# A hybrid RWKV / convolution backbone on one core: priority for three kinds of evictions, and modulation loads behind the last store

## The chip, the cores and the metric

The kernel runs on one core of a Trainium2 chip. The metric is the device time of one execution in microseconds. The engines named below are TensorE (PE in the profile), VectorE (DVE), ScalarE (ACT), GpSimd (POOL) and SyncE (SP, which only issues DMA transfers here).

## The reference

Two layers over 512 latent tokens with a prefix of 256 context tokens, model width 1024. Layer 0 is a time mixing of RWKV-7 kind (16 heads of 64, a scan in both directions) beside a gated short convolution; layer 1 is a Conformer module. Both layers are modulated by a vector that comes from the conditioning. Cut to what matters:

```python
shift, scale, gate = jnp.split(s_lat @ mod_w[i] + mod_b[i], 3, axis=-1)
h = rms_norm(x, g_pre[i]) * (1.0 + scale[:, None]) + shift[:, None]
# layer 0
r, k, v, za, bg, cg, xb, zb = jnp.split(h @ w_in, EVEN_SPLITS, axis=-1)   # context: hc @ w_in
# rwkv_prep: k = k + (centred_shift(k) - k) * mu, and so r, v
def step(S, inp):
    r_t, w_t, k_t, v_t, kk_t, a_t = inp
    sa = jnp.einsum("bhvk,bhk->bhv", S, -kk_t)
    S = (S * w_t[:, :, None, :] + sa[..., None] * (kk_t * a_t)[:, :, None, :]
         + v_t[..., None] * k_t[:, :, None, :])
    return S, jnp.einsum("bhvk,bhk->bhv", S, r_t)
_, S_f, S_b = rwkv_seq(rwkv_prep(hc, rc, kc, vc, *rw), zero, zero, ...)   # context gives the states
ya, _, _ = rwkv_seq(rwkv_prep(h, r, k, v, *rw), S_f, S_b, ...)            # latents start from them
yb = bg * dwconv(cg * xb, sc_w, seg_len)
y = jnp.concatenate([ya * silu(za), yb * silu(zb)], axis=-1) @ w_out
x = x + gate[:, None] * rms_norm(y, g_post[i])
# layer 1: a = u * sigmoid(gl); dwconv of 31 taps; layer_norm; silu(a) * silu(z) @ w_out
```

## The kernel before

The scan is done in chunks of 64 tokens. For each pair of heads (one 128-row block p of the channels) and each direction z, products between keys and receptances within a chunk are made by TensorE into the PSUM tiles `pa` (L677 to L680; `pal` in the profile for latents), and VectorE multiplies them with a mask into `E` (L682). The keys are transposed by TensorE into `pb` and copied by ScalarE into `BKt` (L695). The triangular system within a chunk is solved on VectorE in `solve`: 31 pairs of a product into `xtmp` and a sum into `Y` (L739, L741), each after the last. `merge` (L747 to L766) then puts the inverse together: transposes on VectorE into `kdm` and `am`, two groups of small matmuls into `uh`, and copies into `E`. After that comes the chain (`chain_ctx`, `chain_lat`): a sequence of small dependent steps over the chunks, with matmuls into `zo` and `uh`.

There are 12 stages: s = 0 to 3 run the chains of the context (four blocks, two head pairs each), s = 4 to 11 those of the latents (one head pair each). While the chain of stage s runs, the stage also prepares s + 1 and s + 2: the letters of `STAGE` (L35) name the pieces, S for solve, M for merge, L for the vector work of the preparation (`light`), H for the `pa` and `pb` work (`heavy`), F for fills (projections of receptance and of gate za that lie between the chain's steps; in the latents' stages also the output normalisation `finish`), C for the convolution branch with its gate zb. A scheduler sets the order on each engine: it takes instructions by priority, in the order in which they are written where nothing else is said; `tc.high_priority()` puts an instruction ahead of all others that are ready, and `tc.issue_after(x)` forbids an instruction a place before x. Engines then run their lists strictly in order, and wait at their head.

The projections of the context and latents go through `project` (L443): load two halves of a weight block by SP (`wr` and the block's letters: `wrv`, `wrk`), split each into a high part on ScalarE (`wh`, L129) and a remainder on VectorE (`wl`, L130), then 24 matmuls for the context (`pc...`) and 24 for the latents (`pl...`), which are evicted with the token shift by `shifted`: one ScalarE operation (L437) and two of VectorE (L438, L440). The result of the latents, `lk`, `lv` or `lr`, is stored to the scratch tensor `psp` by a DMA that GpSimd issues (L458).

The modulation of layer 1 and the gate of layer 0 are worked out in the start-up and the first context stages by `rest` (L950 to L976): 17 steps, of which each multiplies four 128x512 pieces of `mod_w` (two matmul columns each, into `uh`, later `mpb`) and then issues the four loads of the step after next, from GpSimd (those of the first steps from SP). The pieces lie in turn in `mwb...` (borrowed from four later tiles; from the ninth step on in `ectx`) and `mwr`. `prep_ctx` calls `rest` after each projection of a block's half, and `lora` (L378), which makes the low-rank decay and rate projections `pwl`, `pal` and `pwc`, after each second of its eight steps.

## Time and profile before

| | |
|---|---|
| median of 3 runs | 1388.19 us (1388.19 to 1389.88) |
| the profiled execution | 1392.7 us, span 1390.9 us |
| mean granted TensorE clock | 0.992 |
| start-up: loads, modulation, first projections, low-rank projections | 0 to about 110 us |
| first context chain to last | up to 482 us |
| latents' chains | from 482 us, some 58 us a stage |
| output projection and layer 1 | to the end |

The profile's page lists busy time by engine, the chain of work that ended last, and the costliest groups of instructions; the trace behind it answers for any stretch. A row of the timeline reads: start, duration, engine, line, operation, tile written <- tiles read, and in brackets the time the engine stood idle before, and what ended it. A row of waits reads: engine, what waited, on what; us in total, times, longest. A row of windows has the busy time and count of PE, weight loads, DVE, ACT and POOL in a stretch, then the granted clock as a share of full speed, the busy share of the DMA engines and GB/s.

### The profile page before, as it was taken

What the parts mean: (1) busy time and instruction counts of PE and PEld (TensorE: products, weight loads), DVE (VectorE), ACT (ScalarE), POOL (GpSimd) and SP (SyncE); (2) the same over time, 40 slices, a digit from 0 to 9 for tenths busy, and PEclk for the clock granted to TensorE, in tenths of its full rate; (3) what the DMA queues carried; (4) which work ended last, traced back from release to release, by engine and by line L of the source; (5) the groups of instructions that cost most, each with busy time, mean ns of one, the idle gap of its engine ahead of it and who ended that gap; (6) DMA issues with size and microseconds to landing.
All of it is one profiled execution on the core that took longest, in us unless ns stands there. A gap on an engine that the chain in (4) does not pass through costs nothing.

```text
span 1390.9 us, 29758 instructions
## 1 busy us (share of the span) xinstructions
PE 1337.1 (96%) x11925; PEld 995.2 (72%) x11925; DVE 985.3 (71%) x2304; ACT 745.3 (54%) x1509; POOL 127.4 (9%) x263
## 2 busy tenths in 40 slices
PE   6989999999899999999999999999999999999998
PEld 2646777777677766676666676677777787788886
DVE  5846879868999599989999998557654653644323
ACT  6536366546756566665666755547742432554222
POOL 4123200001111010101101000010000000000000
PEclk9999999999999999999999999999999999999999
DMA  9855521222323312223222221578621322133232
GB/s 333 254 190 190 189 77 57 87 79 86 88 90 101 99 63 79 70 65 88 82 73 70 76 70 57 183 238 290 222 62 61 121 64 58 61 112 101 91 103 79
DMA packets 139756, 158.55 MB, mean 114 GB/s; under 512 B 15504, under 2 KB 104224, under 8 KB 139498
## 3 DMA queue, kind: packets, MB, share of 16 engines
q1 hardware_dynamic: 123152, 106.47, 24.7%
q0 software_dynamic: 15856, 49.12, 10.8%
q8 instruction: 94, 1.54, 0.5%
q10 hardware_dynamic: 608, 1.06, 0.2%
q14 instruction: 46, 0.37, 0.1%
HBM read 138.33 MB, written 18.28 MB: 113 GB/s over the span
## 4 chain that ended last, share of the span: by engine, by line
PE 66%; DVE 16%; ACT 6%; issue 6%; DMA 5%; SPq 0%; POOL 0%; DVEq 0%; ACTq 0%; POOLq 0%
PE pu L57 10%; PE pz L57 6%; PE f L57 6%; PE uh L57 4%; PE zol L57 4%; PE pcg L57 4%; PE o L57 4%; PE plk L57 3%; PE pxb L57 3%; PE plr L57 2%; PE plv L57 2%; PE pzb L57 2%; DVE E L682 2%; PE pck L57 1%; PE zoc L57 1%
## 5 line engine op out<-in xcount | busy, mean ns | idle before, releaser
L57 PE MATMUL o<-wh,y 128*128 128x512 f32 x248 | 79.7, 397 | 0.0
L739 DVE TENSOR_TENSOR xtmpl<-Xl,Yl 128x126 f32<-128x126 f32 (+22 forms) x248 | 61.9, 250 | 2.8
L741 DVE TENSOR_TENSOR Yl<-Yl,xtmpl 128x126 f32<-128x126 f32 (+22 forms) x248 | 61.9, 250 | 2.7
L1257 ACT CAST ah<-a 64x512 fp32r<-64x512 f32 x32 | 19.8, 618 | 72.6 <-DVE a L1252 72.2
L57 PE MATMUL zol<-UV,E 64*64 64x64 f32 (+1 forms) x1024 | 54.0, 221 | 0.0
L57 PEld LDWEIGHTS o<-wh,y 128*128 128x128 f32 x248 | 45.9, 188 | 9.5
L57 PE MATMUL o<-wl,y 128*128 128x512 f32 x124 | 49.6, 400 | 2.0 <-DVE wl L130 2.0
L57 PE MATMUL pal<-ARl,BKl 64*128 64x128 f32 x512 | 45.7, 298 | 5.8 <-DVE E L682 5.2
L57 PE MATMUL zol<-Hl,ARl 64*64 64x64 f32 x896 | 50.2, 230 | 0.7 <-DVE Hl L854 0.4
L847 ACT COPY UV<-uh 64x128 f32<-64x128 f32 x128 | 33.3, 260 | 32.5 <-PE uh L57 25.0
L57 PEld LDWEIGHTS zol<-Hl,ARl 64*64 64x64 f32 x896 | 34.9, 133 | 20.0 <-issue 15.1
L130 DVE TENSOR_TENSOR wl<-wr,wh 128x1024 fp32r<-128x1024 f32 x28 | 34.2, 1223 | 20.6 <-ACT wh L129 20.5
L57 PEld LDWEIGHTS pal<-ARl,BKl 64*128 64x128 f32 x512 | 36.1, 193 | 16.9 <-issue 10.2
L57 PEld LDWEIGHTS uh<-UV,BKt 128*64 128x64 f32 x704 | 26.3, 137 | 30.3 <-ACT UV L847 23.4
L1252 DVE TENSOR_TENSOR a<-pu,a 128x512 f32<-128x512 f32 x16 | 11.0, 690 | 47.7 <-PE pu L57 45.4
L57 PEld LDWEIGHTS zol<-UV,E 64*64 64x64 f32 (+1 forms) x1024 | 42.2, 136 | 2.8 <-ACT UV L847 2.1
L682 DVE TENSOR_TENSOR E<-pal,maskE 128x512 f32<-128x512 f32 x64 | 43.0, 682 | 0.5 <-PE pal L57 0.3
L1209 DVE SCALAR_TENSOR_TENSOR pr<-px,dbe,What 119x512 f32<-119x512 f32 x32 | 22.6, 747 | 26.6 <-PE px L57 26.6
L129 ACT CAST wh<-wr 128x1024 fp32r<-128x1024 f32 x28 | 29.6, 1057 | 21.3 <-PE o L57 10.7
L854 DVE SCALAR_TENSOR_TENSOR Hl<-uh,PCl,HPl 128x64 f32<-128x64 f32 x112 | 26.4, 277 | 19.4 <-PE uh L57 9.2
L57 PE MATMUL uh<-UV,BKt 128*64 128x64 f32 x704 | 36.3, 232 | 3.3 <-ACT UV L847 2.0
L57 PEld LDWEIGHTS uh<-Ol,E 64*64 64x64 f32 x512 | 19.9, 133 | 24.5 <-ACT Ol L841 17.3
(996 smaller groups left out, 4206.1 us busy)
## 6 DMA issues: line engine op xcount, KB each, us to landing
wr<-in_ev_w_out_dram SPq DMA_DIRECT2D x28, 512.0 KB, 5.2
mwr<-in_mod_w_dram POOLq DMA_DIRECT2D x28, 256.0 KB, 4.3
wrv<-in_ev_w_in_dram SPq DMA_DIRECT2D x16, 256.0 KB, 3.1
ectx<-in_mod_w_dram POOLq DMA_DIRECT2D x16, 256.0 KB, 4.2
wrr<-in_ev_w_in_dram SPq DMA_DIRECT2D x16, 256.0 KB, 2.9
wrza<-in_ev_w_in_dram SPq DMA_DIRECT2D x16, 256.0 KB, 2.8
wrcg<-in_ev_w_in_dram SPq DMA_DIRECT2D x16, 256.0 KB, 2.8
wrxb<-in_ev_w_in_dram SPq DMA_DIRECT2D x16, 256.0 KB, 3.0
```

The lines of the kernel that those rows point to most:

```text
L57: env["pe"] = T.matmul(o, lhsT, rhs, start=start, stop=stop)
L129: S.copy(hi, raw)
L130: env["lo"].tensor_tensor(out=lo, in0=raw, in1=hi, op=ALU.subtract)
L682: st["ev"].append(V.tensor_tensor(out=E[:, h, z * NLAT + c0 : z * NLAT + c0 + m, :], in0=pas[h], in1=maskE[:, z * (1 + h) : z * (1 + h) + ...
L739: V.tensor_tensor(out=tv, in0=X[:, :i, i : i + 1].to_broadcast([P, i, m]), in1=Y[:, i : i + 1, c0:].to_broadcast([P, i, m]), op=ALU.mult)
L741: V.tensor_tensor(out=Y[:, :i, c0:], in0=Y[:, :i, c0:], in1=tv, op=ALU.add)
L847: u_ = S.copy(UV[ZR[1 - h], i : 2 * nch - i : 2 * nch - 1 - 2 * i, ZR[h]], uh[ZR[1 - h], 0:2, :])
L854: h_ = V.scalar_tensor_tensor(out=Hn[:, z, :], in0=uh[:, 2 + z, :], scalar=PC[z][:, i : i + 1], in1=HP[:, z, :], op0=ALU.mult, op1=ALU.add)
L1209: V.scalar_tensor_tensor(out=pr[s][:NPROD], in0=px[s][:NPROD], scalar=dbe[:, 0:1], in1=What[:, n * 512 : n * 512 + 512], op0=ALU.add, op1= ...
L1252: V.tensor_tensor(out=a, in0=pp[1], in1=a, op=ALU.mult)
L1257: S.copy(ahl[s][hr], a[hr])
```

## The change

No instruction is added or taken away on any engine; only their order changes. Four parts:

- Modulation. `lora` leaves out its first call of `rest`, and `prep_ctx` for block 0 makes one more, between the context's and the latents' matmuls of v1. GpSimd's loads for the steps may not be issued before the store of the projection written last (`env["store"]`).
- The evictions of receptance projections (`which` is 0) get high priority.
- The masked evictions into `E` get high priority in the latents' stages.
- The copies into `BKt` get high priority in the latents' stages.

`fills` takes a slice, and a stage letter f would hold later `pa` groups behind a part of the fills. No entry of `STAGE` has an f, so this does nothing.

```diff
@@ lora
-            if kt % 2:
+            if kt % 2 and kt > 1:
                 between()
@@ project
-        shifted(pl, rl, p, which)
-        nc.gpsimd.dma_start(psp[p, which], rl)
+        with nullcontext() if which else tc.high_priority():
+            shifted(pl, rl, p, which)
+        env["store"] = nc.gpsimd.dma_start(psp[p, which], rl)
@@ prep_ctx
-                project(p, which, st[nm][:, cs], inner)
+                project(p, which, st[nm][:, cs], inner if b or (p, which) == (1, 2) else None)
@@ heavy, pa
-                with anchored(an, ha[gi if lat else 2 * gi]):
+                with anchored(an, ha[gi if lat else 2 * gi]), after(st.get("hold") if gi else None):
...
-                        st["ev"].append(V.tensor_tensor(
+                        with tc.high_priority() if lat else nullcontext():
+                            st["ev"].append(V.tensor_tensor(
@@ heavy, pb
-                    st["ev"].append(S.copy(st["BKt"][z][:, :, ZR[h]], pbs[h]))
+                    with tc.high_priority() if lat else nullcontext():
+                        st["ev"].append(S.copy(st["BKt"][z][:, :, ZR[h]], pbs[h]))
@@ rest
-                    nc.gpsimd.dma_start(home(g, q), src)
+                    with tc.issue_after(env["store"].ins):
+                        nc.gpsimd.dma_start(home(g, q), src)
@@
-    sts = [prep_ctx(0, rest)]
+    sts = [prep_ctx(0, rest, inner=rest)]
```

The order on GpSimd in the start-up, before; `lk_559`, `lk_625` and `lv_705` are the latents' projections k0, k1 and v0, whose stores these are:

```order
L976 DMA mwbtanhl_113<-in_mod_w_dram 128x512
L976 DMA mwbtanhl_114<-in_mod_w_dram 128x512
L458 DMA psp<-lk_559 128x512
L976 DMA mwbxal_115<-in_mod_w_dram 128x512
L976 DMA mwbxal_116<-in_mod_w_dram 128x512
L458 DMA psp<-lk_625 128x512
L976 DMA mwr_504<-in_mod_w_dram 128x512
L976 DMA mwr_503<-in_mod_w_dram 128x512
L976 DMA mwr_502<-in_mod_w_dram 128x512
L976 DMA mwr_501<-in_mod_w_dram 128x512
L458 DMA psp<-lv_705 128x512
```

And now:

```order
L459 DMA psp<-lk_559 128x512
L459 DMA psp<-lk_625 128x512
L980 DMA mwbtanhl_113<-in_mod_w_dram 128x512
L980 DMA mwbtanhl_114<-in_mod_w_dram 128x512
L980 DMA mwbxal_115<-in_mod_w_dram 128x512
L980 DMA mwbxal_116<-in_mod_w_dram 128x512
L459 DMA psp<-lv_705 128x512
L980 DMA mwr_504<-in_mod_w_dram 128x512
L980 DMA mwr_503<-in_mod_w_dram 128x512
L980 DMA mwr_502<-in_mod_w_dram 128x512
L980 DMA mwr_501<-in_mod_w_dram 128x512
```

Four loads that stood ahead of and between the two stores of lk now stand behind both, and four more behind the store of lv.

TensorE in the same place, now: the end of the context's matmuls of v1 (`pcv`) and the beginning of the latents' (`plv`); before, the four matmuls on mwb stood behind the 24 of `plv`, right ahead of the four on mwr:

```order
L57 MATMUL pcv_730<-hctx,wlv_726 128x256
L57 MATMUL uh_125<-mwbtanhl_113,s_71 2x512
L57 MATMUL uh_125<-mwbtanhl_114,s_71 2x512
L57 MATMUL uh_125<-mwbxal_115,s_71 2x512
L57 MATMUL uh_125<-mwbxal_116,s_71 2x512
L57 MATMUL plv_766<-hlh_117,whv_719 128x512
L57 MATMUL plv_766<-hll_118,whv_719 128x512
```

One step of the modulation has moved from behind `plv` to ahead of it.

VectorE in a latents' stage (the second), around the last two masked evictions of a head pair, before; `xtmpl` and `Yl` are the solve, `orq` is the output normalisation, and the shape of a solve step shrinks from step to step (here from 5x14 to 4x14):

```order
L741 TENSOR_TENSOR Yl_5628<-Yl_5628,xtmpl_5629 128x5x14
L499 TENSOR_TENSOR orq_5984<-orq_5984 128x8
L682 TENSOR_TENSOR E_4157<-pal_5907,maskE 128x512
L739 TENSOR_TENSOR xtmpl_5629<-Xl_5627,Yl_5628 128x56
L682 TENSOR_TENSOR E_4157<-pal_5906,maskE 128x512
L741 TENSOR_TENSOR Yl_5628<-Yl_5628,xtmpl_5629 128x4x14
```

And now:

```order
L742 TENSOR_TENSOR xtmpl_5629<-Xl_5627,Yl_5628 128x91
L499 TENSOR_TENSOR orq_5984<-orq_5984 128x8
L130 TENSOR_TENSOR wlzb_6148<-wrzb_6146,whzb_6147 128x512
L744 TENSOR_TENSOR Yl_5628<-Yl_5628,xtmpl_5629 128x7x13
L500 TENSOR_TENSOR orq_5984<-orq_5984 128x8
L525 TENSOR_TENSOR lwll_6537<-lwrl_6531,lwhl_6536 128x512
L684 TENSOR_TENSOR E_4157<-pal_5907,maskE 128x512
L684 TENSOR_TENSOR E_4157<-pal_5906,maskE 128x512
```

The two evictions stand next to each other, and the solve has come to its 7x13 step there, where it had come to its 5x14 step before.

## The prediction

> **What bounds the kernel now.** I read the page's busy shares and its chain first, then TensorE's waits stretch by stretch, then the timeline where a wait was long.

> ```profile
> span 1390.9 us, 29758 instructions
> PE 1337.1 (96%) x11925; PEld 995.2 (72%) x11925; DVE 985.3 (71%) x2304; ACT 745.3 (54%) x1509; POOL 127.4 (9%) x263
> PE 66%; DVE 16%; ACT 6%; issue 6%; DMA 5%; SPq 0%; POOL 0%; DVEq 0%; ACTq 0%; POOLq 0%
> ```

> TensorE is busy 96% of the span, and the change leaves its work as it is. So only its idle time (1390.9 - 1337.1 = 53.8 us) and time at a lower clock can be won. Two stretches hold the waits that the edits aim at: the start-up with the context stages, 60 to 482 us, and the latents' stages, 482 to 880 us. After 880 us the order of the work stays. TensorE's waits in the first stretch (total, times, longest):

> ```profile
> PE plv L57 <- DVE lv L440: 4.7, 3, 3.6
> PE pal L57 <- DVE E L682: 3.9, 1, 3.9
> ```

> And in the second:

> ```profile
> PE pbl L657 <- ACT BKt L695: 2.8, 5, 1.0
> PE uh L57 <- DVE aml L748: 2.7, 4, 1.0
> PE pal L57 <- DVE E L682: 1.3, 2, 1.0
> PE pbl L657 <- DVE E L682: 0.6, 2, 0.4
> PE pvl L57 <- ACT BKt L695: 0.4, 1, 0.4
> ```

> **Part 1, the modulation steps at the start.** GpSimd's queue first, then SP's, then how long the value weights' transfers took:

> ```profile
> 62.04 1.09 POOL L976 DMA_DIRECT2D mwbtanhl<-in_mod_w_dram  x2 [12.44 <-PE uh L57]
> 63.13 0.55 POOL L458 DMA_DIRECT2D psp<-lk  x1
> 63.67 1.07 POOL L976 DMA_DIRECT2D mwbxal<-in_mod_w_dram  x2
> 65.11 0.55 POOL L458 DMA_DIRECT2D psp<-lk  x1 [0.38 <-ACT ectx L387]
> ```

> ```profile
> 63.93 1.63 SPq L126 DMA_DIRECT2D wrv<-in_ev_w_in_dram  x2
> ```

> ```profile
> DMA to landing us min/median/max: 3.3/8.0/8.5
> ```

> Four modulation loads and two stores are in flight when the weights of v1 (wrv) are issued. These take 8.0 to 8.5 us, against 3.3 for a wrv later. What follows, in order of time:

> ```profile
> 72.42 0.62 ACT L129 CAST whv<-wrv 128x512 fp32r<-128x512 f32 x1 [5.06 <-DMA wrv<-in_ev_w_in_dram]
> 73.56 2.13 POOL L976 DMA_DIRECT2D mwr<-in_mod_w_dram  x4 [7.90 <-PE uh L57]
> 73.79 13.11 SPq L126 DMA_DIRECT2D wrk<-in_ev_w_in_dram  x4
> 74.30 0.48 PE L57 MATMUL pcv<-hctx,whv 128*128 128x256 f32 x2 [1.02 <-DVE vc L440]
> 78.01 0.62 ACT L129 CAST whk<-wrk 128x512 fp32r<-128x512 f32 x1 [4.11 <-DMA wrk<-in_ev_w_in_dram]
> 78.53 0.68 ACT L437 ACTIVATE lv<-plv,omu 128x512 f32<-128x512 f32 x1
> 80.05 0.75 DVE L440 SCALAR_TENSOR_TENSOR lv<-plv,hmu,lv 128x511 f32<-128x511 f32 x1
> 80.94 0.76 PE L57 MATMUL plv<-hlh,whv 128*128 128x512 f32 x1 [3.56 <-DVE lv L440]
> 81.51 0.63 PE L57 MATMUL plv<-hll,whv 128*128 128x512 f32 x1
> 84.03 0.39 PE L57 MATMUL plv<-hll,whv 128*128 128x512 f32 x1
> 88.00 0.60 PE L57 MATMUL uh<-mwbtanhl,s 128*2 128x512 f32 x2
> 89.83 1.13 PE L57 MATMUL pwl<-ectx,w 128*128 128x512 f32 x2
> ```

> The late wrv holds the cast at 72.42; only then does SP get a buffer for wrk (73.79), which travels beside four mwr loads; ScalarE stands at the cast of wrk until 78.01, and lv's eviction is queued behind it in ScalarE's order. lv frees the PSUM tile that plv(v1) needs. So TensorE idles 1.02 us at pcv and 3.56 us at plv. And it pays a second time, as the granted clock shows:

> ```profile
> 66.00:70.00 4.00, 4.00 (x23) 3.42 (x22) 2.35 (x4) 0.92 (x2) 0.00 (x0) 1.00 0.93 247
> 78.00:82.00 4.00, 1.05 (x3) 0.90 (x4) 2.98 (x5) 1.57 (x3) 0.55 (x1) 0.82 0.74 229
> 82.00:86.00 4.00, 4.00 (x15) 3.21 (x14) 0.19 (x1) 0.62 (x1) 0.00 (x0) 0.75 0.18 66
> ```

> (The last three numbers of a row are granted clock, DMA share and GB/s.) From 80.94 to 84.03 seven matmuls take 3.09 us; the other 17 up to 88.00 take 3.97, 0.233 each, so the seven lose 3.09 - 1.63 = 1.46. A later modulation group waits too:

> ```profile
> 95.19 0.60 PE L57 MATMUL uh<-mwbtanhl,s 128*2 128x512 f32 x2
> 96.44 1.02 PE L57 MATMUL uh<-mwbxal,s 128*2 128x512 f32 x2 [0.21 <-DMA mwbxal<-in_mod_w_dram]
> 97.39 1.12 PE L57 MATMUL pwl<-ectx,w 128*128 128x512 f32 x2
> ```

> It takes 2.20 us; in eight-matmul groups without a wait, as 88.00 with mwr behind it to 89.83, two take 1.83, 0.92 each. So 1.28 is wait. Removable in all: 1.02 + 3.56 + 1.46 + 1.28 = 7.3 us.

> What the changed order does: no load is added, all four move behind the second lk store, to about 65.2 to 67.3. wrv then shares the DMA engines with stores alone. I estimate 3.3 to 5 us for it (above the later wrv's time, below half of 8.5 plus overlap): landed by 69, its subtraction done by 70, wrk issued there rather than at 73.79 and landed by 75 (4.1 us as now, 78.01 less 73.79). lv, two casts' and two shifts' time later (78.01 to 80.80 now, 2.8 us), is through at 77.5. pcv starts when TensorE is free, at 73.28 (74.30 - 1.02). The four matmuls on mwb, now ahead of plv(v1), fill 0.9 us of what was idle; their loads, even at the 8.5 us of the slowest row, are in by 75.8, and the group comes at 76.4 (73.28 and the 3.08 us that pcv takes, from 74.30 to 80.94 - 3.56). So plv(v1) starts near 77.6 at full clock, which leaves 0.3 us idle. The mwr loads now stand behind the store of lv (81.34 now, 77.6 then) in GpSimd's queue instead of ahead of it; with 4 us of travel the last lands near 83.7, when plv(v1) has just ended (77.6 + 24 x 0.233 = 83.2): 0.5 to 1.0 us of new wait, I take 0.8. The loads into ectx further on are also put whole behind stores; bounded by 0 and the 1.28 of the row above, I take 0.3. **Net: -7.3 + 0.3 + 0.8 + 0.3 = -5.9 us**, bounds -7.3 and -2.2 (the last under rival B).

> [...]

> **Part 2, receptance evictions.** 8 fills of one ScalarE and two VectorE operations (0.75 us each by the lv row) move ahead of others in the context stages, where TensorE's order hardly changes. Value 0, bounds -1 and +1.5 (one pair in the way of one chain step).

> **Part 3, the context stage with the 3.9 us wait.** VectorE there:

> ```profile
> 377.50:381.00 3.50, 0.05 (x2) 0.00 (x0) 3.50 (x11) 1.06 (x3) 0.08 (x1) 0.99 0.71 187
> ```

> It is busy all 3.50 us while TensorE waits. Taking the evictions first puts the rest of its queue (the last BK products, then the merge) later by their 4 x 0.68; the wait changes its place rather than goes. Value -0.4, bounds -3.9 and +2.

> **Part 4, the latents' evictions and copies.** The two groups on VectorE:

> ```profile
> L739 DVE TENSOR_TENSOR xtmpl<-Xl,Yl 128x126 f32<-128x126 f32 (+22 forms) x248 | 61.9, 250 | 2.8
> L682 DVE TENSOR_TENSOR E<-pal,maskE 128x512 f32<-128x512 f32 x64 | 43.0, 682 | 0.5 <-PE pal L57 0.3
> ```

> Evictions in pairs, with a solve step (0.25) no longer between, and BKt copies first on ScalarE aim at 2.8 + 1.3 + 0.6 + 0.4 = 5.1 us of waits. Half of these are waits for an operation that starts late for lack of its inputs; I take -2.5. In return the solve is two to three steps (up to six operations, 1.5 us) later at the fourth pair, and TensorE's merges stand later in its order, with fewer zb matmuls (0.23 each) between the last one and the next chain. Where aml is already last (four stages, 2.7 us) more is waited: +1.5, bounds 0 and +10.5 (1.5 in each of seven stages). **Net -1.0.** One more term is the clock:

> ```profile
> 537.00:597.00 60.00, 57.29 (x830) 41.29 (x830) 55.71 (x167) 37.40 (x89) 6.73 (x12) 0.96 0.27 79
> 590.00:592.50 2.50, 2.35 (x94) 2.11 (x96) 2.42 (x5) 1.92 (x4) 0.00 (x0) 1.00 0.17 67
> 592.50:599.00 6.50, 6.50 (x126) 5.89 (x121) 5.28 (x16) 3.75 (x8) 0.00 (x0) 0.51 0.28 83
> ```

> Here no wait was over 1.0 us (the longest of pbl on BKt), yet after a run of transposes, two merges and the output's transposes, without a zb matmul (128x512) between, the clock was 0.51 for 6.5 us: up to 6.5 x 0.49 = 3.2 us. In the new order such a run is gone from this stage and comes together in another. Value 0, bounds -3.2 and +3.2 for each further stage.

> [...]

> **The sum:** -5.9 + 0 - 0.4 - 1.0 = -7.3 us. The profiled execution took 1392.7 us (1.8 around its span), 4.5 above the median of 1388.19; I take the same difference off the median: 1380.9.

> **The rivals.** A, more is won: the 5.1 us all go, the merges have cover (in most stages aml is ready before TensorE comes), the low clock of 592 us does not come again: -5.9 - 5.1 - 3.2 = -14.2, 1374. Against it: VectorE is busy 55.71 of 60 us in that row, so it has little room.

> B, the loads collide all the same: the second wrv is issued by 65.6 (63.93 + 1.63), just as the four loads now start, the DMA engines were busy 0.93 of the time with this traffic (row 66.00:70.00), and if that wrv still lands near 73 and wrk with it, lv stays where it is. Then only the group's 0.92 in the idle time and the 1.28 are won: -2.2, and with part 4 unsure, 1386: no change that can be told. [...] For the forecast speaks that pcv begins with the first half of the weights, issued before the loads.

> C, slower: the solve becomes what TensorE waits for. Place: the merge (aml, then E) ahead of the next chain in seven stages; price 1.5 us a stage, 10.5 in all, with Part 1 won: -5.9 + 10.5 = +4.6, 1392.8. It outweighs the start-up from 5.9/7 = 0.84 us a stage. For it: VectorE's 93% in the stage above. Against: the waits for aml are 0.7 on average now and the merges are scheduled later with it.

> D, the clock halves in two further latents' stages: -7.3 + 6.4 = -0.9, 1387.3.

> **How the numbers follow.** Chances: forecast 0.50, A 0.14, B 0.16, D 0.06, C 0.14. A measurement tells 0.2%, 2.8 us. The forecast (1377 to 1385) and A are faster: 0.64; B and D same: 0.22; C slower: 0.14. The range leaves out the outer part of A and most of C: 1373.5 to 1391.

> **What would show it.** Right: wrv under 6 us, plv(v1) within 1 us of the modulation group at clock 1.0, the chain of the first context stage 5 to 6 us earlier; waits of pbl and pal on BKt and E halved, those on aml up. Wrong: wrv still at 8 us (B), waits on aml over 8 us in all or chain starts waiting for E (C), clock rows near 0.5 in other latents' stages (D).

## The result, and the profile after

| | before | changed |
|---|---|---|
| median of 5 runs | 1388.19 us (1383.39 to 1390.31) | 1399.02 us (1395.87 to 1401.13) |
| profiled execution, span | 1392.7, 1390.9 us | 1400.05, 1398.3 us |
| mean granted clock | 0.992 | 0.989 |

The ratio is 1.0075, with a 95% interval of 1.0048 to 1.0102: slower by about 10.8 us, where 7.3 us less were forecast. (Ratios, here and below, compare the fast executions of both kernels and are not quotients of the medians shown.) The page of the changed kernel, span, busy time by engine and chain:

```profile
span 1398.3 us, 29732 instructions
PE 1345.5 (96%) x11925; PEld 999.3 (71%) x11925; DVE 986.1 (71%) x2304; ACT 742.8 (53%) x1509; POOL 127.1 (9%) x263
PE 71%; DVE 12%; ACT 7%; issue 5%; DMA 4%; POOL 0%; SPq 0%; DVEq 0%; ACTq 0%; POOLq 0%
```

TensorE is busy 8.4 us longer (1337.1 before) with the same matmuls: some of them ran slower. The start-up went largely as foreseen. The changed kernel's timeline, with SP's issue of wrv, ScalarE's cast of wrk and the moved modulation group:

```profile
63.43 1.63 SPq L126 DMA_DIRECT2D wrv<-in_ev_w_in_dram  x2
...
73.66 0.62 ACT L129 CAST whk<-wrk 128x512 fp32r<-128x512 f32 x1 [4.16 <-DMA wrk<-in_ev_w_in_dram]
...
75.73 0.60 PE L57 MATMUL uh<-mwbtanhl,s 128*2 128x512 f32 x2
```

The transfers of wrv, and the window that stood at 0.82 of the clock before:

```profile
DMA to landing us min/median/max: 2.8/3.3/3.8
```

```profile
78.00:82.00 4.00, 4.00 (x19) 3.32 (x18) 0.69 (x1) 0.62 (x1) 3.77 (x8) 1.00 0.85 281
```

wrv lands in 2.8 to 3.8 us instead of 8.0 to 8.5, the cast of wrk comes 4.35 us earlier, and TensorE is busy throughout this window at full clock. The first group on ectx begins at 117.48 instead of 123.68. But that is the last good news. The group on mwr right behind plv, and two later groups on ectx, each of which takes 1.04 us where it waits for nothing, wait for loads:

```profile
82.39 2.59 PE L57 MATMUL uh<-mwr,s 128*2 128x512 f32 x8
...
130.44 2.34 PE L57 MATMUL mpb<-ectx,s 128*2 128x512 f32 x8
...
161.29 2.06 PE L57 MATMUL mpb<-ectx,s 128*2 128x512 f32 x8
```

And TensorE's waits in the latents' stages, 482 to 886 us:

```profile
PE uh L57 <- DVE aml L751: 4.9, 5, 1.5
PE pal L57 <- DVE E L684: 3.1, 7, 1.1
PE pbl L658 <- DVE E L684: 2.1, 5, 0.7
PE pbl L658 <- ACT BKt L698: 1.8, 4, 0.7
PE uh L57 <- ACT UV L850: 1.6, 6, 0.4
PE uh L57 <- DVE Pml L764: 1.3, 2, 0.7
PE po L57 <- DVE Ol L890: 1.0, 4, 0.4
```

The waits on BKt fell from 2.8 to 1.8, but those on E, whose priority was raised, rose from 1.3 + 0.6 to 3.1 + 2.1, and those on the merge's inputs (aml, Pml) from 2.7 to 6.2. The timelines of VectorE and TensorE show both in one stage:

```profile
640.96 0.16 DVE L499 TENSOR_TENSOR orq<-orq 128x8 f32<-128x8 f32 x1
642.19 0.75 DVE L927 SCALAR_TENSOR_TENSOR yb<-cx,hcol,yb 128x512 f32<-128x512 f32 x1 [1.07 <-ACT yb L925]
642.86 1.28 DVE L684 TENSOR_TENSOR E<-pal,maskE 128x512 f32<-128x512 f32 x2
...
644.19 1.16 PE L57 MATMUL pal<-ARl,BKl 64*128 64x128 f32 x16 [1.14 <-DVE E L684]
...
652.40 0.18 DVE L744 TENSOR_TENSOR Yl<-Yl,xtmpl 128x16 f32<-128x16 f32 x1
652.50 2.02 DVE L736 STREAM_TRANSPOSE Xl<-Nt 128x1024 f32<-128x1024 f32 x1
654.40 1.01 DVE L750 STREAM_TRANSPOSE kdml<-Yl 128x512 f32<-128x512 f32 x1
655.45 0.71 DVE L751 STREAM_TRANSPOSE aml<-kdml 128x512 f32<-128x512 f32 x1
...
656.22 1.53 PE L57 MATMUL uh<-aml,E 32*32 32x32 f32 x64 [1.54 <-DVE aml L751]
```

The pair of evictions stands right behind yb, which waits 1.07 us for ScalarE: high priority gave it a place in the order, not a way past a waiting head, and TensorE waits 1.14 us for E. And the solve ends at 652.40, so late that the next solve's 2.0 us transpose Xl stands ahead of the merge; TensorE waits 1.54 us for aml there. The whole of the latents, from the first chain's start to the last one's, before and changed (sums over the seven stages; the first two numbers are length and TensorE's busy time):

```profile
sum 396.00, PE 381.73 PEld 269.83 DVE 358.06 ACT 245.51 POOL 39.01; mean PE 54.53 PEld 38.55 DVE 51.15 ACT 35.07 POOL 5.57
```

```profile
sum 403.70, PE 385.87 PEld 272.11 DVE 358.74 ACT 243.61 POOL 38.93; mean PE 55.12 PEld 38.87 DVE 51.25 ACT 34.80 POOL 5.56
```

Of the 7.7 us more, idle time is 17.83 - 14.27 = 3.6; the other 4.1 are busy time, most of it at a lower clock. Windows of the changed kernel, in pairs:

```profile
537.35:540.75 3.40, 2.13 (x70) 1.65 (x71) 2.84 (x7) 3.12 (x6) 0.77 (x2) 1.00 0.28 83
540.75:544.15 3.40, 3.40 (x36) 1.78 (x38) 2.75 (x6) 1.29 (x3) 0.37 (x1) 0.50 0.29 100
653.40:656.80 3.40, 1.86 (x55) 1.32 (x49) 3.32 (x5) 1.90 (x4) 0.57 (x1) 1.00 0.28 81
656.80:660.20 3.40, 3.40 (x46) 2.85 (x40) 3.08 (x7) 2.83 (x5) 0.56 (x1) 0.50 0.28 95
```

In both pairs 3.40 us at full clock, in which TensorE was busy 63 and 55% of the time, are followed by 3.40 us at 0.50 of it. After 482 us the changed kernel has four of these (540.75, 656.80, 769.45, 834.30, each 3.4 us), the kernel before one of 6.85 us (592.55). Counting half of such time as lost, that is 6.8 against 3.4: +3.4 us. So 3.6 + 3.4 of the 7.7 are accounted for. A ledger of the two profiled executions, by marks on TensorE, in us:

| stretch | before | changed | |
|---|---|---|---|
| up to the first group on ectx | 123.7 | 117.5 | -6.2 |
| to the third context chain (s = 2) | 158.9 | 163.5 | +4.6: among it a new half-clock stretch of 6.85 us at 247.2 (3.4) and the groups on ectx (1.3 + 1.0) |
| to the fourth (s = 3) | 129.1 | 128.3 | -0.8 |
| to the first latents' chain | 70.7 | 73.4 | +2.7: idle 1.7 to 4.0 |
| the latents' chains | 396.0 | 403.7 | +7.7 |
| the rest, to the end of the span | 512.5 | 511.9 | -0.6 |

### The profile page after: what moved, and what is told of

It is laid out like the page before. It is cut to its first block, busy times and chain, and to the rows that moved or that the text cites. A ratio compares the mean times of both kernels' runs of the same rounds, so it can differ in the third digit from the quotient of the medians.

```text
span 1398.3 us, 29732 instructions
## 1 busy us (share of the span) xinstructions
PE 1345.5 (96%) x11925; PEld 999.3 (71%) x11925; DVE 986.1 (71%) x2304; ACT 742.8 (53%) x1509; POOL 127.1 (9%) x263
## 3 DMA queue, kind: packets, MB, share of 16 engines
q10 hardware_dynamic: 608, 1.06, 0.2%
## 4 chain that ended last, share of the span: by engine, by line
PE 71%; DVE 12%; ACT 7%; issue 5%; DMA 4%; POOL 0%; SPq 0%; DVEq 0%; ACTq 0%; POOLq 0%
PE pu L57 13%; PE pz L57 6%; PE f L57 6%; PE uh L57 5%; PE zol L57 4%; PE pxb L57 4%; PE pcg L57 3%; PE plk L57 3%; PE plv L57 3%; PE pzb L57 2%; PE o L57 2%; PE pza L57 2%; DMA wr<-in_ev_w_out_dram 2%; PE plr L57 1%; PE pck L57 1%
## 5 line engine op out<-in xcount | busy, mean ns | idle before, releaser
L57 PE MATMUL o<-wh,y 128*128 128x512 f32 x248 | 79.6, 397 | 0.0
L57 PE MATMUL zol<-UV,E 64*64 64x64 f32 (+1 forms) x1024 | 54.2, 222 | 0.1
L57 PEld LDWEIGHTS o<-wh,y 128*128 128x128 f32 x248 | 46.0, 188 | 9.5
L57 PE MATMUL pal<-ARl,BKl 64*128 64x128 f32 x512 | 44.6, 296 | 7.8 <-DVE E L684 3.8
L57 PE MATMUL zol<-Hl,ARl 64*64 64x64 f32 x896 | 50.2, 230 | 0.7 <-DVE Hl L857 0.6
L57 PE MATMUL o<-wl,y 128*128 128x512 f32 x124 | 49.5, 399 | 1.3 <-DVE wl L130 1.3
L57 PEld LDWEIGHTS zol<-Hl,ARl 64*64 64x64 f32 x896 | 35.0, 133 | 20.4 <-issue 16.5
L57 PEld LDWEIGHTS pal<-ARl,BKl 64*128 64x128 f32 x512 | 35.0, 191 | 18.9 <-DVE E L684 9.7
L57 PEld LDWEIGHTS uh<-UV,BKt 128*64 128x64 f32 x704 | 26.4, 137 | 28.5 <-ACT UV L850 23.1
L57 PEld LDWEIGHTS zol<-UV,E 64*64 64x64 f32 (+1 forms) x1024 | 42.6, 137 | 2.4 <-ACT UV L850 2.0
L129 ACT CAST wh<-wr 128x1024 fp32r<-128x1024 f32 x28 | 29.6, 1057 | 20.7 <-DMA wr<-in_ev_w_out_dram 10.4
L57 PE MATMUL uh<-UV,BKt 128*64 128x64 f32 x704 | 36.3, 232 | 2.1 <-ACT UV L850 1.6
L57 PEld LDWEIGHTS uh<-Ol,E 64*64 64x64 f32 x512 | 20.0, 133 | 25.0 <-ACT Ol L844 18.9
```

Of the source, the lines that this page charges most:

```text
L57: env["pe"] = T.matmul(o, lhsT, rhs, start=start, stop=stop)
L129: S.copy(hi, raw)
```

## The experiments

Every time is a median against the kernel before on the same chip, which stood at 1386.6 to 1387.7 us. Theory 1 was at first: the masked evictions are the loss, since they push the solve back. Rival theories: the receptance evictions (2), and half-clock stretches that any shift moves about (3).

### One part of the change at a time

```diff
e1, the modulation's hunks:
+            if kt % 2 and kt > 1:
+        env["store"] = nc.gpsimd.dma_start(psp[p, which], rl)
+                project(p, which, st[nm][:, cs], inner if b or (p, which) == (1, 2) else None)
+                    with tc.issue_after(env["store"].ins):
+    sts = [prep_ctx(0, rest, inner=rest)]
e2, project:  +        with nullcontext() if which else tc.high_priority():
                  shifted(pl, rl, p, which)
e3, heavy:    +        with tc.high_priority() if lat else nullcontext():
                  st["ev"].append(V.tensor_tensor(out=E[...], ...))
e4, heavy:    +        with tc.high_priority() if lat else nullcontext():
                  st["ev"].append(S.copy(st["BKt"][z][:, :, ZR[h]], pbs[h]))
```

> The modulation part alone (steps moved, loads behind stores). Theory 1 (the masked evictions cost the loss): 5 to 7 us faster than before, 1381 to 1383, the group on mwr after pck at 107 us as in the changed kernel (113 before) and every later chain start 5 to 6 us earlier than before. Theory 2 (the receptance evictions cost it): the same. Theory 3 (episodes of the halved clock, which any shift in time moves about, cost it): the start-up gain is there up to 200 us, but the total is anywhere from -7 to +3, by how many episodes of 3.4 us or more the execution meets (the changed kernel met seven after 60 us, before three).

> High priority for the receptance evictions alone. Theory 1: within 2 us of before. Theory 2: 4 us or more slower, and lost between 200 and 482 us, where the changed kernel gave back its 6 us. Theory 3: within 4 us either way, with the loss, if any, equal to half the time at the halved clock.

> High priority for the latents' masked evictions alone. Theory 1: 6 to 12 us slower, of it 5 to 9 between the first and last latents' chain start; TensorE's waits on aml and E up from 4.6 us to 9 or more. Theory 2: within 2 us of before. Theory 3: within 4 us, waits as before, and the difference equals the halved clock.

> High priority for the BKt copies alone. Theory 1 and 2: within 2 us of before, the waits of pbl on BKt below the 2.8 us of before. Theory 3: within 4 us either way. If it is 5 us or more slower, none of the three holds and the copies displace the chain's copies on ScalarE.

| run | median us | ratio | interval |
|---|---|---|---|
| e1, modulation | 1387.89 | 0.9996 | 0.9975 to 1.0017 |
| e2, receptance | 1390.11 | 1.0020 | 1.0001 to 1.0040 |
| e3, masked evictions | 1399.27 | 1.0096 | 1.0074 to 1.0118 |
| e4, key copies | 1392.31 | 1.0050 | 1.0032 to 1.0069 |

The masked evictions alone lose as much as the whole change (11.7 us between the medians, against 10.8); theory 2 falls. The key copies lose 4.8 us, which no theory gave, and the waits of pbl on BKt, which were to fall below 2.8, are at 2.9. The modulation part, worth 5 to 7 us by expectation, measures nothing. And the four do not add up (19 us against 10.8). e3 loses in its first stages. In e3, the stage ahead of the first latents' chain, up to that chain's second step, and the first latents' stage from there to the second chain; then two windows in the latter:

```profile
411.50:488.10 76.60, 72.69 (x706) 55.85 (x705) 56.20 (x125) 43.02 (x87) 7.43 (x14) 0.96 0.32 93
488.10:551.90 63.80, 58.71 (x757) 41.69 (x756) 56.03 (x167) 36.93 (x90) 6.72 (x12) 0.92 0.24 72
523.80:527.20 3.40, 1.16 (x16) 0.97 (x16) 3.40 (x10) 0.81 (x2) 0.00 (x0) 1.00 0.02 5
527.20:534.00 6.80, 6.21 (x39) 4.85 (x39) 6.53 (x27) 2.47 (x4) 0.00 (x0) 0.50 0.26 77
```

Between the same steps these two took 72.4 and 56.3 before, so 4.2 and 7.5 are lost. In the second, TensorE waits at two groups of pal that the scheduler put next to each other:

```profile
524.75 1.16 PE L57 MATMUL pal<-ARl,BKl 64*128 64x128 f32 x16 [1.21 <-DVE E L683]
527.79 2.08 PE L57 MATMUL pal<-ARl,BKl 64*128 64x128 f32 x16 [1.88 <-DVE E L683]
```

One wide matmul stands between the second and third group of that stage in its order, and none between third and fourth, where the kernel before has 10 and 7. That order leaves no time for the evictions between the groups; VectorE, busy all 3.40 us of the window, came to them late, and 6.8 us at half the clock followed. The loss in the first of the two has a mark of its own:

```profile
438.77 0.45 PE L57 MATMUL zol<-h,ARl 64*64 64x64 f32 x8
...
441.65 1.90 PE L57 MATMUL pal<-ARl,BKl 64*128 64x128 f32 x16 [2.20 <-ACT BKl L633]
```

The first step of the first latents' chain, at 482.41 before, has moved 44 us ahead. Behind it TensorE waits 2.20 us, and 3.4 us at half the clock follow from 441.88 on. In all, five of the kernels here have this step at 439 to 446 us (e3, and below e6, e10, e11 and e12), the others at 475 to 483; these five, and no other, have a half-clock stretch between 411 us and the second step. No run moves this step alone, so what it costs by itself is not shown.

### Without the masked evictions, with the solve, and by stages

```diff
e5: the change without high_priority at E[...]
e6: e3, and in solve
+            with tc.high_priority() if st["lat"] else nullcontext():
                 V.tensor_tensor(out=tv, ...)
                 V.tensor_tensor(out=Y[:, :i, c0:], ...)
e7: e3 with  tc.high_priority() if lat and st["p"] >= 3 else nullcontext()
e8: e1 with  tc.issue_after(env["store"].ins) if g < 8 else nullcontext()
```

> The change without the priority of the masked evictions. Theory 1 (the masked evictions are the loss, 9 to 12 us of it): within 4 us of before, latents' stages 58 us each as before. Theory 2 (the three priorities cost as they did alone, and add up): 5 to 9 us slower. Theory 3 (each order loses by chance to waits and to the episodes of halved clock that they set off): no rule, but the time is that of the shortest order plus idle time plus half of the episodes.

> Masked evictions alone, with the same high priority for the solve steps of the latents. Theory 1a (the solve pushed back by the evictions is what TensorE waits for, in the merges): waits on aml below 3 us in all and most of the 11.7 us gone, 1388 to 1392. Theory 1b (TensorE's own order is what loses: the evictions end earlier in the scheduler's reckoning, groups that need them are put earlier than the chip has them ready): waits on E, BK and the chain stay, 1396 to 1402.

> Masked evictions alone, but only for the head pairs from the fourth on (prepared in the third latents' stage and later). With priority for all, the stretch from the context's last but one chain to the end of the first latents' stage lost 16 us against before (133.4 + 76.6 + 63.8 against 129.1 + 70.7 + 58.0) and the later stages 2.6. So by theory 1 and by the stages' rows: within 3 us of before, the stretch up to the third latents' chain as before.

> The modulation part alone, with the loads behind the store only for the first eight steps (those into mwb and mwr at the start), not for those into ectx. The part alone had no effect: its start-up was 1 to 2 us ahead at the fourth load step (119.0 against 119.1 to 120.6 in three other runs of the old order), and two groups on ectx took 1.8 and 2.2 us instead of 1.04. If these loads behind stores are what gives the gain back: groups on ectx 1.04 again, 1.9 us faster than the part alone, 1384 to 1386. If not: 1387 to 1389.

e5: 1388.96, ratio 1.0014 (1.0002 to 1.0026). Without the masked evictions 8 to 9 of the 10.8 us are gone, and e2 and e4 do not add. e6: 1392.00, 1.0032 (1.0006 to 1.0058): the solve's priority takes back about 7 of e3's 11.7 us, and the waits on aml, here with the stage ahead of the latents, fall from e3's 4.2 us to

```profile
PE uh L57 <- DVE aml L750: 0.6, 2, 0.4
```

That fits 1a, though not all of it: TensorE's waits for E fall too, at pal from 4.6 to 0.9 us. e7: 1388.07, 1.0020 (1.0004 to 1.0035): with the first three pairs left out the loss nearly goes. e8: 1386.78, 1.0021 (1.0004 to 1.0038), a miss as a total, though the groups on ectx were at 1.04 us again, but for one of 1.31.

### The solve with the whole change, and alone

```diff
e9:  the change, and the solve's high_priority as in e6
e10: e3 with  tc.high_priority() if lat and st["p"] < 3 else nullcontext()
e11: before, and the solve's high_priority
e12: e8, and the solve's high_priority
```

> The whole change with the latents' solve steps at the same high priority. Theory 1a (TensorE waits in the merges for a solve that the prioritised work pushed back): waits on aml in the latents below 2 us (4.9 in the changed kernel), and half or more of the 10.8 us back, 1388 to 1394. Theory 1b (TensorE's own order is what loses): waits on E, BKl and BKt stay at 9 us or more and the time within 3 us of the changed kernel's 1399.

> The complement of the run with priority from the fourth head pair on: masked evictions at high priority for the first three pairs only. If the loss sits where their stages' rows put it (context's last two stages and the first latents' stage, +16 us in that execution, and little later): 9 to 13 us slower, 1396 to 1400. If every stage loses its share: 3/8 of 11.7, 4 to 5 us slower.

> High priority for the latents' solve steps alone, nothing else of the change. Theory 1a gives the 2.7 us of waits on aml, and no more: 1384 to 1387. If any priority on VectorE in these stages loses (theory 3): 1389 or more, with episodes of halved clock after 372 us that the run of before does not have.

> The version for a better time: modulation steps with loads behind stores for the first eight only, and the solve steps at high priority. Theory 1a: the two together, 1383 to 1386 against 1386.6 of before. If the start-up gain cannot be told and the solve's priority moves waits elsewhere: within 3 us of before.

e9: 1387.09, 0.9988 (0.9968 to 1.0008). One more priority takes back all of the loss, some 12 us. e10: 1397.39, 1.0075 (1.0046 to 1.0104): the loss of the masked evictions lies at the first three pairs, as e7 said. e11: 1401.15, 1.0089 (1.0058 to 1.0119), and e12: 1395.51, 1.0063 (1.0044 to 1.0083): misses, and the most telling ones. The solve's priority, which mends the change, loses as much when it stands alone as the evictions' does. Waits in the latents' stages, first e3, then e11, then e9:

```profile
PE pal L57 <- DVE E L683: 4.6, 6, 1.9
PE uh L57 <- DVE aml L749: 3.5, 4, 1.4
```

```profile
PE pal L57 <- DVE E L682: 4.3, 6, 2.0
...
PE uh L57 <- DVE aml L749: 0.4, 1, 0.4
```

```profile
...
PE pbl L658 <- DVE E L684: 2.2, 4, 0.6
PE pbl L658 <- ACT BKt L698: 2.1, 5, 0.5
...
PE uh L57 <- DVE aml L752: 0.6, 1, 0.6
...
PE pal L57 <- DVE E L684: 0.2, 1, 0.2
```

Evictions and solve share VectorE, and TensorE needs both. With the evictions' priority alone, aml gets later (3.5 us against 2.7 before) and pal's E does too (4.6 against 1.3); with the solve's alone, aml falls to 0.4 and pal's E rises to 4.3. With both, these two waits come to 0.8 us together, against 4.0 before. Not all gets better: pbl's wait for E is 2.2 us against 0.6, and all of TensorE's waits in the latents are 12.2 us in e9 against 13.4 before and 16.7 in the changed kernel. Nor is the evictions' priority the only one that delays aml: in e4 and in e5, where they have none and the key copies have it, that wait is 4.7 us.

One stage shows what the time is made of. It is the one ahead of the first latents' chain, from the fourth context chain to the second step of that chain; idle is length less TensorE's busy time:

| run | length | idle | at half clock | busy |
|---|---|---|---|---|
| before | 72.4 | 1.7 | 0 | 70.7 |
| changed | 75.1 | 4.0 | 0 | 71.1 |
| e3, masked | 76.6 | 3.9 | 6.8 | 72.7 |
| e4, key copies | 74.5 | 3.7 | 0 | 70.8 |
| e9, change and solve | 71.8 | 0.9 | 0 | 70.8 |
| e11, solve | 76.4 | 3.5 | 6.8 | 72.9 |

Where the clock was full, TensorE's busy time is the same within 0.4 us in every order; the two orders with 6.8 us at half the clock are busy some 2 us longer. All that an order changes here is waits, and the half clock that comes behind some of them. So theory 3 holds in part: half-clock stretches are a share of these losses, but they come where an order has brought a wait.

### The modulation part, in an order that loses nothing

```diff
e13: e9 without the hunks of e1
e14: e9 with  tc.issue_after(env["store"].ins) if g < 8 else nullcontext()
```

> The three priorities with the solve's, without the modulation part. If that part is worth what the prediction put on it, 6 us slower than with it (1387), 1393; if it is worth nothing in the total (start-up gain 2, given back at the groups on ectx), 1386 to 1388, with groups on ectx of 1.04 us and a start-up stretch from the first to the last modulation group within 1 us of the 115.3 in the middle of six runs of the old order.

> The change with the solve's priority, and with the loads behind the store only for the first eight steps. TensorE's and VectorE's orders are those of the run with the solve's priority, so only GpSimd's queue differs. If the groups on ectx cost the 1.9 us that their rows show: 1385 to 1386 against 1387, and faster than before by 0.1 to 0.2%. If not: within 1 us of 1387.

e13: 1387.42, 0.9994 (0.9978 to 1.0011). e14: 1385.23, 0.9977 (0.9961 to 0.9993), the one version that is faster than the kernel before, by some 3 us (a small difference, but its interval leaves out 1). In e14 the groups on ectx are at 1.04 us again:

```profile
128.97 1.04 PE L57 MATMUL mpb<-ectx,s 128*2 128x512 f32 x8
...
147.81 1.04 PE L57 MATMUL mpb<-ectx,s 128*2 128x512 f32 x8
```

From the start of the modulation group at 60.72 to that of the last one, at 179.10 (in the execution before), the start-up took, over all profiles: old order, nine executions, 114.3 to 118.7 us, median 115.4; the change's order, four, 114.2 to 115.9, median 115.2; first eight only, three (e8, e12, e14), 112.5 to 114.2, median 113.1. By the medians the part is worth 0.2 us as made, 2.3 with ectx left alone. The totals bear this out in one order and not in the other. e14 and e13, on the same chip, differ in this part alone (with ectx left alone), and the means of their executions by 2.7 us. But alone (e8) it was not measured as a gain: the interval, 1.0004 to 1.0038, leaves out 2.3 us less (0.9983). Eight executions of e8 took 1384.3 to 1387.4 us, four 1393.0 to 1394.3 at a mean clock of 0.987 to 0.989, against 0.992 to 0.996 in the eight; the clock outweighs the part there.

## Why the prediction was wrong

**Part 1, mechanism right, sizes wrong.** wrv in under 6 us, pcv and plv without their waits, full clock: each step came out, and against the execution before the first mark was 6.2 us earlier. But the sum rested on that one execution. Of nine executions of the old order's start-up three had the half-clock stretch near 80 us, and they are the three longest (117.0, 118.4, 118.7), with the three longest waits at plv (2.64, 3.56, 3.68 us); the other six wait 1.7 to 2.4 us there and keep their clock. The hint was there: the profiled execution lay 4.5 us above the median, and the terms that made it so were counted as removable. Two more sizes were too small. The new wait on mwr, put at 0.8, is 2.59 - 1.04 = 1.55 us (1.2 to 2.6 in the seven profiles of the new order). The loads into ectx behind stores, put at 0.3, cost 1.3 + 1.0.

**Part 2**, put at 0 with bounds -1 and +1.5: measured +2.8 (0.1 to 5.5). The term rested on TensorE's order hardly changing in the context stages. The trace of e2 shows a place, in the first of them, where it does: plv now stands ahead of a merge that it stood behind.

```profile
248.13 0.77 PE L57 MATMUL plv<-hlh,whv 128*128 128x512 f32 x1 [1.35 <-DVE lv L440]
```

The wait for lv was 0.56 us there before. In e2 6.85 us at half the clock begin at 247.8, and so they do in the changed kernel, at 247.2.

**Part 3** held: -0.8 against -0.4, and the wait at pal went from 3.90 us for E to 2.80 us for BKl, so it changed its place rather than went, as foreseen.

**Part 4 failed.** The step that takes -2.5 of the 5.1 us of waits on E and BKt as won is the wrong one: the waits on E rose by 3.3 us, those on BKt fell by 1.0. The evictions got an earlier place in VectorE's order, but on the chip that queue ran late (the row at 642.19), and TensorE waited longer for it. The merges, put at +1.5, took 3.5 (2.7 to 6.2). And the clock, put at 0, took 3.4. Rivals C and D were both named, with chances of 0.14 and 0.06, as alternatives. Here they came together: within the 3.41 us ahead of the half clock at 540.75, 656.80 and 769.45 us TensorE waits 1.27, 1.54 and 1.08 us for aml, and ahead of that at 834.30 us 0.72 us for Pml and 0.36 for Ol. C's price of 1.5 us for each of seven stages was too high for the wait alone; its direction was right.

**D's mechanism was wrong in one point.** Part 4's term for the clock, from which D comes, took a run of short matmuls and transposes as the cause, since in the row 590.00:592.50 TensorE was busy 94% of the time just ahead of the low clock. That row begins behind the wait of 1.03 us on BKt. The whole 3.4 us ahead, in the kernel before:

```profile
589.15:592.55 3.40, 2.47 (x96) 2.22 (x97) 3.29 (x7) 2.77 (x6) 0.00 (x0) 1.00 0.32 82
```

Here it was busy 73%. And the changed kernel has such a run, merges and transposes without a wide matmul:

```profile
712.10:718.80 6.70, 5.81 (x208) 5.23 (x208) 6.36 (x15) 4.30 (x8) 0.53 (x1) 1.00 0.19 47
```

TensorE was busy 87% of it and kept its clock. In the 16 profiles of this study 55 half-clock stretches began between 60 us and TensorE's last matmul, and in the 3.41 us ahead of each TensorE was busy at most 79% of the time. Little busy time alone did not bring it: 144 other steps of 3.41 us at full clock (9 in the kernel before, 10 in the changed one) were as little busy, and the clock stayed. So idle time, at least 21% of the step, was there each time, and the short matmuls from 712.10 on, with 13% of it, kept the clock. What transposes alone do to the clock is not shown: of the run at 712.10 only the 16 matmuls of pbl, about 1.0 us, are issued as transposes (L658); po, pvl and the merges are plain matmuls.

What stays open: why the key copies alone cost 4.8 us. They put idle time into the stage ahead of the latents (3.7 for 1.7: waits on the chain's UV, on aml, E and Pml), bring the wait on aml to 4.7, and the stretch at half the clock near 590 us lasts 10.2 us instead of 6.85; how a priority on ScalarE delays VectorE's aml was not traced. Nor was why lv comes later with the receptance evictions' priority.

## What to carry to other kernels

A high priority for one of two streams that share an engine can delay the other, and here even its own (in e3 TensorE's waits on aml rose from 2.7 to 3.5 us, those of pal on E from 1.3 to 4.6), and the engine that needs both loses; raise all that it waits for, or none, and measure each alone. A saving read from one profiled execution should be checked against how that execution lies among the timed ones, above all where transfers are in it (wrv landed in 6.8 to 8.5 us in the nine executions of the old order). Here a wait could cost twice: behind the three longest of the changed kernel's five waits on aml in the latents, 1.08 to 1.54 us, came 3.4 us each at half the clock.
